# A hybrid decoder step: where squares, sampled states and recurrence chunks stand in the order

## The chip, the cores and the metric

The kernel runs on one core of a Trainium2 chip. The time is device microseconds (us) of one execution, from the first to the last instruction and what lies around them; a run is given by its median. A core has five engines that work side by side, each through its own instructions in a fixed order: TensorE (PE: matmuls and transposes), VectorE (DVE), ScalarE (ACT), GpSimd (POOL) and SyncE (SP, which issues most of the transfers). POOL and ACT issue transfers too.

## The reference

One layer of a hybrid decoder on 512 prompt tokens and 8 sampled tokens, width 1024, in float32. One combined projection of the normalised input feeds two branches: a retention (4 heads, keys of 256, values of 512, chunks of 128 tokens) and an RWKV-7 time mixing (16 heads of 64). Each branch has a SiLU gate and its own down projection; sigmoid gates merge them.

```python
h = _rmsnorm(x, norm_g)
P = einsum('btd,dn->btn', concat([h_prev, h]), w_in)[:, 1:]     # all projections
# retention, per head; s0 is zero for the prompt, state_ret for the samples
inner = einsum('bhid,bhjd->bhij', qc, kc) * dmask
o = einsum('bhij,bhjv->bhiv', inner, vc) + einsum('bhid,bhdv->bhiv', qc * q_dec, s)
s = chunk_dec * s + einsum('bhjd,bhjv->bhdv', kc * k_dec, vc)
# RWKV-7, per token
sk = einsum('bhvk,bhk->bhv', s, kk_t)
s = s * w_t - sk * (a_t * kk_t) + v_t * k_t
o = einsum('bhvk,bhk->bhv', s, r_t)
```

After the merge follow an output projection and residual, a per-layer embedding with a gate, and a final norm. The outputs are the tokens, both branches' new states and the shift rows.

## The kernel before, in words

**Products.** Activations and weights are split into a high and a low half (`hhi`/`hlo`, `whi`/`wlo`, `yahi`/`yalo`, `ybhi`/`yblo`), and each product is three matmuls: high by high, high by low, low by high. A weight comes by SP into `raw` (three buffers, L142), ACT copies it to `whi` (L147) and DVE subtracts for `wlo` (L148); `whi` and `wlo` have two buffers each, so a new copy waits until PE has done with the weight before the last one. `mm_half` (L160) runs the matmuls over one half of the tokens (256 or 264 columns) into a PSUM tile `ph`, one of four.

**Stages.** (1) Prologue: the four token tiles `xt` of 128 tokens and the samples' `xs` are squared by ACT (`sumsq`, L263), the inverse root is taken by 13 small DVE instructions (`inv`, L178 to L186), the rows are scaled (L270), transposed by PE (L278) and split (L282, L283), tokens 0 to 255 by `transposed(0)`, the rest by `transposed(1)`. (2) The RWKV projections and what the recurrence needs, pair of heads by pair (to 262 us). (3) The four retention heads (to 707 us): keys and queries with rotation (`rx`, L801), values (`phv`, L838, with the samples' `vsm`, L831), scores, the gates `gs` (L891), `sampled(h)`, the outputs. `sampled(h)` loads the 8 samples' states of a head in four tiles `tS` of 1 MB by POOL (L758), scales them by the decay on ACT (L764, 16 copies), adds the new outer product on DVE (L765), reads them by PE (L770) and stores them. (4) The RWKV recurrence, 8 chunks of 64 tokens, each a chain over all engines: products `UO` (L1025), the solve `U` (L1034), the state's step `dS` (L1040), `UO` again (L1043), the outputs `Ot` copied by ACT (L1056). Between the chunks' steps lie *fills*: eight merge gates `mg` (stored to MBd by SP) and then eight output tiles of the first down projection, `down_a` (weights of the retention's output `ya`; results `ua`, stored to UAd). (5) The second down projection, down_b, on the recurrence's output: `yb` is written to YBd tile by tile, loaded again by SP (L1149) when stage 5 begins, and split (L1150, L1151). (6) Output projection, embedding, final norm.

**What sets the order.** The program is written out once; a scheduler then simulates the engines and lays each engine's instructions in an order, by priorities (`tc.high_priority(offset=...)`, a larger offset goes first) and by `tc.issue_after(i)`, which lets nothing in its block be taken up before instruction `i` in the order. `after(a, b)` is a true dependency. On the chip, each engine then keeps the order it was given, whatever comes late. In stage 4 the table `AT` says how many fills have been written by the time chunk c is: chunk c follows fill number AT[c].

Of the kernel before, what the change touches and what calls it, by code (L numbers as in the profile page):

```python
# [8 lines left out]
F32 = mybir.dt.float32  # L9
F32R = mybir.dt.float32r  # L10
I32 = mybir.dt.int32
AF = mybir.ActivationFunctionType
# [5 lines left out]
T, B8, NT = 512, 8, 520  # L18
# [7 lines left out]
DV = 512  # L26
# [53 lines left out]
def body(tc, A, O, dbg=None, upto="Z"):  # L80
# [3 lines left out]
    act, dve, pe, sp, pool = nc.scalar, nc.vector, nc.tensor, nc.sync, nc.gpsimd  # L84
# [7 lines left out]
    with es:  # L92
# [51 lines left out]
        def weights(src, keep=None, ready=None):  # L144
            raw, ld = ready or fetch(src)
            hi, lo = keep or [wp.tile([128, KT, 128], F32R, tag=t, name=t, bufs=2) for t in ("whi", "wlo")]
            cp = act.activation(hi, raw, AF.Copy)  # L147
            sb = dve.tensor_tensor(lo, raw, hi, ALU.subtract)  # L148
            marks[:] = [getattr(i, "ins", i) for i in (ld, sb, cp)]
            return hi, lo  # L150
# [110 lines left out]
        def sumsq(x, r_, n):  # L261
            junk = p0.tile([128, D], F32, tag="junk", name="junk", bufs=2)
            act.activation(junk[0:r_], x, AF.Square, accum_out=ssq[0:r_, n:n + 1])  # L263
# [8 lines left out]
        def transposed(g):  # L272
            for q in range(4):
                ps = (bank("pht") if q < 3 else pq.tile([128, 512], F32, tag="po", name="pht")).rearrange("p (k t) -> p k t", k=2)
                for n in range(2):
                    for i in range(2):
                        k = 2 * q + i
                        pe.transpose(ps[:, i, n * 128:(n + 1) * 128], xts[2 * g + n][:, k * 128:(k + 1) * 128], ident)  # L278
                for i in range(2):
                    k = 2 * q + i  # L280
                    cs = slice(256 * g, 256 * g + 256)
                    hi = act.activation(hhi[:, k, cs], ps[:, i], AF.Copy, scale=ng[:, k:k + 1])  # L282
                    last = dve.scalar_tensor_tensor(hlo[:, k, cs], ps[:, i], ng[:, k:k + 1], hhi[:, k, cs], ALU.mult, ALU.subtract)  # L283
            return [getattr(i, "ins", i) for i in (hi, last)]
# [6 lines left out]
        with tc.issue_after(getattr(last, "ins", last)):  # L291
            pre = [weights(None, ready=raws[0])]
        with tc.high_priority(offset=10000):
            sumsq(xs[0:8], 8, 4)
            for n in (2, 3):
                sumsq(xts[n], 128, n)
            with tc.issue_after(getattr(last, "ins", last)):
                inv(2, 5)
                scaled(xts[2], 128, 2, act)
                scaled(xts[3], 128, 3)  # L300
                scaled(xs[0:8], 8, 4)
        last = transposed(0)
        with tc.issue_after(last[0]), tc.issue_after(last[1]):
            pre.append(weights(None, ready=raws[1]))
        ps = bank("phs")
        psv = ps[:, 0:KT * 16].rearrange("p (k b) -> p k b", b=16)
        for k in range(KT):
# [437 lines left out]
        dve.tensor_tensor(s8, s8, i4[:, 2], ALU.add)  # L745
        dve.tensor_tensor(sum8, s8, i4[:, 3], ALU.add)

        def sampled(h):
            qz = pR.tile([128, 2, 4, 34], F32, tag="qz", name="qz", bufs=1)
            dve.memset(qz, 0.0)  # L750
            dve.tensor_copy(qz[:, :, :, 0], qs[:, h, :, 0:4])
            dve.tensor_copy(qz[:, :, :, 33], qs[:, h, :, 4:8])
            po = pq.tile([128, 512], F32, tag="po", name="po")
            for g in range(2):
                Ss = []
                for i in range(2):
                    S = pT.tile([128, 4, NT], F32, tag="tS", name="tS", bufs=4)[:, :, 0:DV]
                    pool.dma_start(S, A["state_ret"][0, 4 * g:4 * g + 4, h, 128 * i:128 * i + 128, :].rearrange("b p v -> p b v"))  # L758
                    Ss.append(S)
                for b in range(4):  # L760
                    vb = bank("vb")
                    pe.matmul(vb, sel[:, 4 * g + b, :], vsr, start=True, stop=True)  # L762
                    for i, S in enumerate(Ss):
                        act.activation(S[:, b, :], S[:, b, :], AF.Copy, scale=GAM[h])  # L764
                        last = dve.scalar_tensor_tensor(S[:, b, :], vb, ks[:, h, i, 4 * g + b:4 * g + b + 1], S[:, b, :], ALU.mult, ALU.add)  # L765

                for i, S in enumerate(Ss):
                    n_ = 32 if g == 0 and i == 0 else 2
                    for b in range(4):
                        m_ = pe.matmul(po[32 * b:32 * b + n_, :], qz[:, i, b, 32 * g:32 * g + n_], S[:, b, :],  # L770
                                       start=(n_ == 32), stop=(g == 1 and i == 1), skip_group_check=True)
                        if b == 0 and i == 0:
                            after(m_, last)
                    pool.dma_start(O[5][0, 4 * g:4 * g + 4, h, 128 * i:128 * i + 128, :].rearrange("b p v -> p b v"), S)
            return po

        def sampled_out(h, po):
# [6 lines left out]
            for i in range(4):  # L784
# [3 lines left out]
                              ps.rearrange("p (i b r) -> p i b r", i=4, b=4)[:, :, :, 0:2],  # L788
                              gs8[:, hs_, :].rearrange("p i (g b) -> p i b g", g=2), ALU.mult)

        OFF = [0, 512, 896, 1152]
        GBC = [0, 0, 0, 4, 8]
        for h in range(H):
# [33 lines left out]
            for j in range(4):  # L827
                ready = fetch(w_in[256 * j:256 * j + 256, O_V + DV * h:O_V + DV * h + DV])
                raws, w = raws[-1:] + [wide(ready[0])], [wide(t) for t in weights(None, ready=ready)]
                if j % 2:  # L830
                    ms = [pe.matmul(vsm[32 * g:32 * g + 32], hst[:, 2 * j - 2 + g, :], raws[g // 2][:, g % 2, :],  # L831
                                    start=(j == 1), stop=(j == 3), skip_group_check=True) for g in range(4)]
                    side_by_side(ms)
                    after(ms[0], marks[2])
                for jt in range(4):
                    for k in range(2):
                        for x, (w_, r) in enumerate(((w[0], hhi), (w[0], hlo), (w[1], hhi))):
                            m_ = pe.matmul(vps[jt], r[:, 2 * j + k, 128 * jt:128 * jt + 128], w_[:, k, :],  # L838
                                           start=(j == 0 and k == 0 and x == 0), stop=(j == 3 and k == 1 and x == 2))
                tail[:] = [getattr(m_, "ins", m_)]  # L840
                advance("v")
            vhi = pB.tile([128, 4, DV], F32R, tag="vhi", name="vhi")
            vlo = pB.tile([128, 4, DV], F32R, tag="vlo", name="vlo")
# [35 lines left out]
            for jt in range(4):  # L879
# [2 lines left out]
                    pe.transpose(ps[:, 128 * i:128 * i + 128], kf[i][:, 128 * jt:128 * jt + 128], ident)  # L882
                act.activation(dhi[:, jt, :], ps[:, 0:256], AF.Copy, scale=kdec[:, h, jt:jt + 1])
                dve.scalar_tensor_tensor(dlo[:, jt, :], ps[:, 0:256], kdec[:, h, jt:jt + 1], dhi[:, jt, :], ALU.mult, ALU.subtract)
            po = sampled(h)

            gs = []
            for i in range(4):
                g = pB.tile([128, NT], F32, tag="vg", name="gs", bufs=4)
                for (j, c0, c1), ps in zip(HV, proj(w_in[:, col(O_GA + DV * h, i)], hhi, hlo)):  # L890
                    act.activation(g[:, c0:c1], ps, AF.Silu)  # L891
                act.activation(gs8[:, 4 * h + i, :], g[:, T:NT], AF.Copy)
                gs.append(g)
                advance("gate")
                if h == H - 1 and i == 2:
                    ya_tiles(h, pT)
                    ya_load(0, pT, pool)
# [199 lines left out]
            loads(1)  # L1097
        done = []
        nxt_y = beside_rwkv(128, slice(0, 128))
        AT = [0, 3, 6, 8, 9, 11, 12, 13, 16]  # L1100
        for c in range(NCH):
            with tc.high_priority(offset=20000):
                PS = chunk(c)
            if c % 2 == 1:
                x = (Ot, 128, slice((c - 1) * C, (c + 1) * C))
                with tc.high_priority(offset=10000):
                    finish_rwkv(*x)
                done.append((c + 1, x))
            for _ in range(AT[c + 1] - AT[c]):
                next(fl)  # L1110
            if c + 2 < NCH:
                with tc.issue_after(marks[0]), tc.high_priority(offset=20000):
                    loads(c + 2)
            if done and c == done[0][0]:
                with tc.high_priority(offset=10000):
                    emit_rwkv(*done.pop(0)[1], *nxt_y)
                nxt_y = beside_rwkv(128, slice(c * C, c * C + 128)) if c != 4 else beside_rwkv(B8, slice(T, NT))
            if c == 4:
                o8 = pC.tile([128, 16, C], F32, tag="Ot", name="o8", bufs=2)[0:B8]
                pool.dma_start(o8, OSd.rearrange("(b h) v -> b h v", h=16))  # L1120
                x = (o8, B8, slice(T, NT))
                finish_rwkv(*x)
                emit_rwkv(*x, *nxt_y)
                nxt_y = beside_rwkv(128, slice(c * C, c * C + 128))
# [205 lines left out]
```

## Time and profile before

| | |
|---|---|
| median of 3 runs | 1075.98 us (1072.61 to 1078.3) |
| profiled execution | 1071.51 us, span 1069.7 us |
| PE busy | 1042.0 us of the span, 97% |
| mean granted clock of PE | 0.992 |
| weight copies `whi` on ACT / `wlo` on DVE | 135 x 1.06 us / 135 x 1.22 us |
| transfers | 199.45 MB, 186 GB/s over the span |

A row of the time line has the start, the length, the engine (SPq is SP's queue of transfers), the line of the kernel, what is written from what, the shapes, the count and, in brackets, how long the engine stood idle before and what released it. PE is busy nearly everywhere, so what counts is where it stands idle, and how the engines that feed it are ordered just before.

### The profile page before, as it was taken

The numbers are of one execution on the slowest core, as the hardware profiler recorded it, in microseconds if no ns is written. First come the engines' busy times: TensorE is split into PE (matmuls) and PEld (weight loads), VectorE is DVE, ScalarE is ACT, GpSimd is POOL, SyncE is SP. The second block draws the span as 40 slices with busy tenths as digits, with TensorE's granted clock in tenths as the row PEclk, the third lists the DMA queues.
The fourth block names the chain that finished last, engine by engine and source line by source line (L and its number), as shares of the span: only waits on it lengthen the run. The fifth ranks groups of instructions, "written<-read, shape, count | busy, mean of one in ns | idle before, by whom it ended". The sixth has DMA issues, their size and how long they took to land.

```text
span 1069.7 us, 22049 instructions
## 1 busy us (share of the span) xinstructions
PE 1042.0 (97%) x8932; PEld 974.8 (91%) x8932; DVE 785.2 (73%) x1429; ACT 494.8 (46%) x973; POOL 79.5 (7%) x139
## 2 busy tenths in 40 slices
PE   7999999999999999999999999998999999999995
PEld 6999989999879788987989889898999999999995
DVE  6647989884499699949894698864777755666875
ACT  6744565544464543373445333354323224334554
POOL 2000110100300200010010000110001100000000
PEclk8999999999999999999999999999999999999998
DMA  5623488788943943493288633969996649643222
GB/s 182 179 80 99 122 191 223 188 246 228 330 160 90 327 146 99 144 319 103 86 310 229 230 115 112 328 198 330 309 283 214 171 145 302 206 119 100 81 59 81
DMA packets 239224, 199.45 MB, mean 186 GB/s; under 512 B 58988, under 2 KB 203225, under 8 KB 237970
## 3 DMA queue, kind: packets, MB, share of 16 engines
q1 hardware_dynamic: 225586, 149.60, 47.7%
q0 software_dynamic: 13376, 48.17, 13.2%
q8 instruction: 70, 1.15, 0.4%
q14 instruction: 32, 0.26, 0.1%
q10 hardware_dynamic: 160, 0.27, 0.1%
HBM read 137.70 MB, written 60.00 MB: 185 GB/s over the span
## 4 chain that ended last, share of the span: by engine, by line
PE 85%; DMA 6%; DVE 3%; ACT 2%; issue 1%; SPq 1%; POOL 0%; DVEq 0%; POOLq 0%; ACTq 0%
PE ph L160 58%; PE phv L838 8%; PE o L910 3%; PE st L921 2%; PE sc L863 1%; PE po L770 1%; PE g L506 1%; PE UO L1025 1%; DMA raw<-in_w_ple_gate_dram 1%; DMA raw<-in_w_in_dram 1%; DMA yalo<-YAd 1%; DMA BKt<-BKd 1%; DMA MBd<-mg 1%; PE vb L762 1%; PE vsm L831 1%
## 5 line engine op out<-in xcount | busy, mean ns | idle before, releaser
L160 PE MATMUL ph<-hhi,whi 128*128 128x256 f32 (+2 forms) x1296 | 370.5, 286 | 0.9 <-ACT hhi L282 0.4
L160 PE MATMUL ph<-hlo,whi 128*128 128x256 f32 (+2 forms) x1296 | 369.4, 285 | 0.2 <-DVE hlo L283 0.2
L160 PE MATMUL ph<-hhi,wlo 128*128 128x256 f32 (+2 forms) x1296 | 368.8, 285 | 0.5 <-DVE wlo L148 0.5
L160 PEld LDWEIGHTS ph<-hhi,whi 128*128 128x128 f32 x1296 | 244.2, 189 | 6.1 <-issue 1.7
L160 PEld LDWEIGHTS ph<-hhi,wlo 128*128 128x128 f32 x1296 | 245.0, 189 | 2.2 <-DVE wlo L148 0.7
L160 PEld LDWEIGHTS ph<-hlo,whi 128*128 128x128 f32 x1296 | 244.5, 189 | 1.9 <-DVE hlo L283 0.7
L147 ACT ACTIVATE whi<-raw 128x1024 fp32r<-128x1024 f32 x135 | 142.9, 1059 | 208.9 <-PE ph L160 154.2
L148 DVE TENSOR_TENSOR wlo<-raw,whi 128x1024 fp32r<-128x1024 f32 x135 | 164.8, 1221 | 86.4 <-ACT whi L147 85.4
L160 PE MATMUL ph<-yalo,whi 128*128 128x256 f32 (+1 forms) x256 | 72.4, 285 | 0.0
L160 PE MATMUL ph<-yahi,whi 128*128 128x256 f32 (+1 forms) x256 | 72.2, 284 | 0.0
L160 PE MATMUL ph<-yahi,wlo 128*128 128x256 f32 (+1 forms) x256 | 71.9, 285 | 0.0
L623 DVE TENSOR_TENSOR tm<-M 128x62 f32<-128x62 f32 (+30 forms) x62 | 52.9, 853 | 0.6
L625 DVE TENSOR_TENSOR M<-M,tm 128x62 f32<-128x62 f32 (+30 forms) x62 | 52.8, 852 | 0.6
L838 PE MATMUL phv<-whi,hhi 128*128 128x512 f32 x128 | 51.5, 403 | 0.0
L838 PE MATMUL phv<-whi,hlo 128*128 128x512 f32 x128 | 50.5, 395 | 0.0
L160 PEld LDWEIGHTS ph<-yalo,whi 128*128 128x128 f32 x256 | 48.1, 188 | 0.3
L160 PEld LDWEIGHTS ph<-yahi,whi 128*128 128x128 f32 x256 | 48.1, 188 | 0.2
L160 PEld LDWEIGHTS ph<-yahi,wlo 128*128 128x128 f32 x256 | 47.8, 188 | 0.3
L838 PE MATMUL phv<-wlo,hhi 128*128 128x512 f32 x128 | 46.8, 395 | 0.5 <-DVE wlo L148 0.5
L765 DVE SCALAR_TENSOR_TENSOR tS<-vb,ks,tS 128x512 f32<-128x512 f32 x64 | 44.1, 742 | 3.3 <-PE vb L762 3.3
L764 ACT ACTIVATE tS<-tS 128x512 f32<-128x512 f32 x64 | 35.0, 620 | 12.5 <-DMA tS<-in_state_ret_dram 12.4
L215 ACT ACTIVATE mg<-ph 128x256 f32<-128x256 f32 (+1 forms) x48 | 17.7, 378 | 41.2 <-PE ph L160 20.6
(454 smaller groups left out, 2120.0 us busy)
## 6 DMA issues: line engine op xcount, KB each, us to landing
raw<-in_w_in_dram SPq DMA_DIRECT2D x97, 512.0 KB, 5.0
tS<-in_state_ret_dram POOLq DMA_DIRECT2D x16, 1024.0 KB, 8.4
out_dram<-tS POOLq DMA_DIRECT2D x16, 1024.0 KB, 9.9
KR<-KRd SPq DMA_DIRECT2D x8, 1024.0 KB, 9.5
raw<-in_w_down_a_dram SPq DMA_DIRECT2D x16, 512.0 KB, 6.8
KRd<-KRS SPq DMA_DIRECT2D x16, 256.0 KB, 4.5
KRd<-GM SPq DMA_DIRECT2D x16, 256.0 KB, 4.8
BKt<-BKd SPq DMA_DIRECT2D x8, 512.0 KB, 9.9
```

The lines of the kernel that those rows point to most:

```text
L147: cp = act.activation(hi, raw, AF.Copy)
L148: sb = dve.tensor_tensor(lo, raw, hi, ALU.subtract)
L160: m_ = pe.matmul(ps[:, 0:c1 - c0], w[:, k, :], r[:, k0 + k, c0:c1], start=(x == 0), stop=(x == n_ - 1))
L215: act.activation(g[:, c0:c1], ps, fn, scale=scale)
L506: ms = [pe.matmul(gs[2 * q + hh][:, c * 128:(c + 1) * 128], BK[hs_, 4 * q + c, :], KRS[hs_, 4 * q + c, :], start=True, stop=True) for q in ...
L623: dve.tensor_tensor(tv, M[:, 0:s, s:s + 1].to_broadcast([128, s, n]), M[:, s:s + 1, s + 1:C].to_broadcast([128, s, n]), ALU.mult)
L625: dve.tensor_tensor(M[:, 0:s, s + 1:C], M[:, 0:s, s + 1:C], tv, ALU.add)
L764: act.activation(S[:, b, :], S[:, b, :], AF.Copy, scale=GAM[h])
L765: last = dve.scalar_tensor_tensor(S[:, b, :], vb, ks[:, h, i, 4 * g + b:4 * g + b + 1], S[:, b, :], ALU.mult, ALU.add)
L838: m_ = pe.matmul(vps[jt], r[:, 2 * j + k, 128 * jt:128 * jt + 128], w_[:, k, :], start=(j == 0 and k == 0 and x == 0), stop=(j == 3 and k ...
L910: pe.matmul(ps, a_[:, o_:o_ + 128], b_[:, jt, :], start=(x == 0), stop=(x == len(seq) - 1))
L921: pe.matmul(ps, a_[:, jt, 128 * i:128 * i + 128], b_[:, jt, :], start=(x == 0), stop=(x == 11))
```

## The change

**A, prologue.** `transposed(0)` for tokens 0 to 255 is written, with priority, ahead of the squares of the other tokens and the samples. These squares come after its last ACT split (`last[0]`), their inverse root and scaling after its last DVE split (`last[1]`), and the second weight is split after both.

**B, sampled states.** `sampled(h)` is divided: `sampled_states(h)` issues the loads, `sampled(h, SS)` does the rest. Head 0's loads depend on PE's products with V's second and fourth weight (`vmark`), and its work is written behind the first gate's copy of the sampled columns. For the other heads the two stand one behind the other as before.

**C, recurrence.** `AT` goes from [0, 3, 6, 8, 9, 11, 12, 13, 16] to [0, 6, 8, 9, 10, 11, 12, 13, 16], and each chunk but the first may be taken up only behind the last matmul of the fills written before it (`tail[0]`).

```diff
         with tc.high_priority(offset=10000):
-            sumsq(xs[0:8], 8, 4)
+            last = transposed(0)
+        with tc.issue_after(last[0]), tc.issue_after(last[1]):
+            pre.append(weights(None, ready=raws[1]))
+        with tc.high_priority(offset=9000), tc.issue_after(last[0]):
             for n in (2, 3):
                 sumsq(xts[n], 128, n)
-            with tc.issue_after(getattr(last, "ins", last)):
+            sumsq(xs[0:8], 8, 4)
+            with tc.issue_after(last[1]):
                 inv(2, 5)
                 scaled(xts[2], 128, 2, act)
                 scaled(xts[3], 128, 3)
                 scaled(xs[0:8], 8, 4)
-        last = transposed(0)
-        with tc.issue_after(last[0]), tc.issue_after(last[1]):
-            pre.append(weights(None, ready=raws[1]))
...
-        def sampled(h):
+        def sampled_states(h):
+            Ss = []
+            for g in range(2):
+                for i in range(2):
+                    S = pT.tile([128, 4, NT], F32, tag="tS", name="tS", bufs=4)[:, :, 0:DV]
+                    ld = pool.dma_start(S, A["state_ret"][0, 4 * g:4 * g + 4, h, 128 * i:128 * i + 128, :].rearrange("b p v -> p b v"))
+                    if h == 0:
+                        after(ld, vmark[g])
+                    Ss.append(S)
+            return Ss
...
+                if j % 2:
+                    vmark.append(m_)
...
-            po = sampled(h)
+            SS = sampled_states(h)
+            if h:
+                po = sampled(h, SS)
...
-                act.activation(gs8[:, 4 * h + i, :], g[:, T:NT], AF.Copy)
+                a_ = act.activation(gs8[:, 4 * h + i, :], g[:, T:NT], AF.Copy)
                 gs.append(g)
+                if h == 0 and i == 0:
+                    with tc.issue_after(getattr(a_, "ins", a_)):
+                        po = sampled(h, SS)
...
-        AT = [0, 3, 6, 8, 9, 11, 12, 13, 16]
+        AT = [0, 6, 8, 9, 10, 11, 12, 13, 16]
         for c in range(NCH):
-            with tc.high_priority(offset=20000):
+            with ExitStack() as cs_:
+                if c:
+                    cs_.enter_context(tc.issue_after(tail[0]))
+                cs_.enter_context(tc.high_priority(offset=20000))
                 PS = chunk(c)
```

What this makes of the engines' orders is seen at three places. Line numbers of the changed kernel are up to 19 higher.

ACT in the prologue, `-` as it was and `+` as it is now; `junk` are the squares, `hhi` the split of `transposed(0)`, `whi` the copy of the second weight:

```order
+L282 ACTIVATE hhi<-pht,ng 128x256 x8
+L263 ACTIVATE junk,ssq<-xt 128x1024 x2
+L147 ACTIVATE whi<-raw 128x1024
 L263 ACTIVATE junk,ssq<-xs 8x1024
-L263 ACTIVATE junk,ssq<-xt 128x1024 x2
-L282 ACTIVATE hhi<-pht,ng 128x256 x8
-L147 ACTIVATE whi<-raw 128x1024
 L270 ACTIVATE xt<-xt,rs 128x1024
```

The eight splits now stand ahead of the squares, and one square stands behind the second weight's copy.

ACT in the V products of head 0, as it was; `rx` is the copy of a key's or query's product, `whi` in the third row from the end the copy of V's second weight, which `vsm` and the products behind it wait for:

```order
L801 ACTIVATE rx<-ph 128x256
L764 ACTIVATE tS<-tS 128x512 x4
L147 ACTIVATE whi<-raw 128x1024
L801 ACTIVATE rx<-ph 128x264
L764 ACTIVATE tS<-tS 128x512 x8
```

and now, first at the same place, then behind the first gate's copy of the sampled columns (`gs_66<-gs`):

```order
L810 ACTIVATE rx<-ph 128x256
L147 ACTIVATE whi<-raw 128x1024
L810 ACTIVATE rx<-ph 128x264
L822 ACTIVATE qhi<-m_3894 128x512
L824 ACTIVATE qs<-m_3894 128x8
...
L905 ACTIVATE gs_66<-gs 128x8
L772 ACTIVATE tS<-tS 128x512 x15
L894 ACTIVATE dhi<-kt,kdec 128x256
L772 ACTIVATE tS<-tS 128x512
L904 ACTIVATE gs<-ph 128x256
L879 ACTIVATE ihi<-s__4152 128x128
L147 ACTIVATE whi<-raw 128x1024
```

The scalings of the states have left the V products and stand, all 16, between the first gate and the copies of the second gate and of the next weight.

SP where down_a ends and down_b begins, as it was; `raw` are down_b's weights, `ua` and `UAd` down_a's tiles, `yb` the recurrence's output:

```order
L142 DMA raw<-in_w_down_b_dram 128x8x128
L1074 DMA ua<-MAd 128x520
L142 DMA raw<-in_w_down_b_dram 128x8x128
L1149 DMA yb<-YBd 128x8x128
L1077 DMA UAd<-ua 128x520
L1149 DMA yb<-YBd 128x8x128 x2
L1149 DMA yb<-YBd 128x8x8
L1161 DMA xn<-in_x_prompt_dram 128x512 x2
```

and now:

```order
L142 DMA raw<-in_w_down_b_dram 128x8x128
L1090 DMA ua<-MAd 128x520
L142 DMA raw<-in_w_down_b_dram 128x8x128
L1093 DMA UAd<-ua 128x520
L142 DMA raw<-in_w_down_b_dram 128x8x128 x2
L1093 DMA UAd<-ua 128x520
L142 DMA raw<-in_w_down_b_dram 128x8x128
L1168 DMA yb<-YBd 128x8x128 x3
L1168 DMA yb<-YBd 128x8x8
L1180 DMA xn<-in_x_prompt_dram 128x512 x2
```

The loads of `yb` stand behind the store of down_a's last tile and behind the third, fourth and fifth weight of down_b. On PE the number of down_a's matmuls between the second transpose `so` (the recurrence's final state) and down_b has gone from 135 to 17; between chunk 7's last `UO` and down_b from 353 to 233. Ahead of chunk 1's `UO` there are now 48 matmuls of the merge gates, where there were none.

More of the change, by code (lines that the diff above doesn't have):

```diff
@@ L746, in body, with sampled @@
         dve.tensor_tensor(sum8, s8, i4[:, 3], ALU.add)
-        def sampled(h):
+        def sampled_states(h):
[8 more added lines that the diff above has]
+            return Ss
+        def sampled(h, SS):
             qz = pR.tile([128, 2, 4, 34], F32, tag="qz", name="qz", bufs=1)
@@ L754, in sampled @@
             for g in range(2):
[L755 to L759, printed above, removed]
+                Ss = SS[2 * g:2 * g + 2]
                 for b in range(4):
@@ L789, in sampled_out @@
                               gs8[:, hs_, :].rearrange("p i (g b) -> p i b g", g=2), ALU.mult)
+        vmark = []
         OFF = [0, 512, 896, 1152]
```

## The prediction

> **What bounds the kernel now.** I read the busy times first, then the chain that ended last, then the list of what TensorE waited for. The page's busy times and chain:
>
> ```profile
> PE 1042.0 (97%) x8932; PEld 974.8 (91%) x8932; DVE 785.2 (73%) x1429; ACT 494.8 (46%) x973; POOL 79.5 (7%) x139
> PE 85%; DMA 6%; DVE 3%; ACT 2%; issue 1%; SPq 1%; POOL 0%; DVEq 0%; POOLq 0%; ACTq 0%
> ```
>
> TensorE (PE) is busy 1042.0 of 1069.7 us, so an edit can win only from the 27.7 us in which PE does nothing, and it loses whatever new idle time it makes. The waits of PE, by line and releaser (us in total, times, longest):
>
> ```profile
> PE UO L1025 <- ACT Ot L1056: 3.4, 3, 2.7
> PE vsm L831 <- issue: 2.6, 1, 2.6
> PE g L506 <- ACT a L455: 1.4, 2, 0.7
> PE g L506 <- ACT sg L455: 1.1, 1, 1.1
> ```
>
> Three edits, five places: I go through them in order of time, each against the profiled execution.
>
> **1. The prologue (edit A): +1.3 us.** ScalarE (ACT), VectorE (DVE) and PE rows of the prologue:
>
> ```profile
> 10.76 1.04 ACT L263 ACTIVATE junk<-xt 128x1024 f32<-128x1024 f32 x1
> 11.80 3.13 ACT L282 ACTIVATE hhi<-pht,ng 128x256 fp32r<-128x256 f32 x8
> 14.79 1.08 ACT L147 ACTIVATE whi<-raw 128x1024 fp32r<-128x1024 f32 x1
> 18.29 1.15 ACT L270 ACTIVATE xt<-xt,rs 128x1024 f32<-128x1024 f32 x1 [2.41 <-DVE rs L186]
> 15.91 1.23 DVE L148 TENSOR_TENSOR wlo<-raw,whi 128x1024 fp32r<-128x1024 f32 x1
> 17.05 0.15 DVE L184 TENSOR_TENSOR nt<-rs 128x3 f32<-128x3 f32 x1
> 18.03 0.16 DVE L186 SCALAR_TENSOR_TENSOR rs<-nt,rs 128x3 f32<-128x3 f32 x1
> 21.28 0.60 PE L278 MATMUL pht<-ident,xt 128*128 128x128 f32 x4
> ```
>
> Before, the squares (junk) end at 11.8 and hhi runs to 14.9. DVE's steps of the inverse root slip in between the hlo copies, the last six from 17.05 to 18.03, 0.2 us apart; the ACT scaling of token tile 2 ends at 19.44, before PE asks for it at 21.28. With the new order ACT runs hhi when its transposes come (about 11.55 to 14.7), then two squares (2 x 1.0, to 16.6), then the second whi (1.08, to 17.7), then the sample's square (to 18.8). Only then can DVE start the inverse root: 13 instructions of some 0.2 us, to 21.4; the scaling takes 1.15, to 22.55. PE's transposes of tokens 2 and 3 start at 22.6 in place of 21.28: **+1.3**. Bounds: +0.4, if the 13 steps take the 0.15 us of their rows (0.65 less) and the squares start 0.25 sooner; +2.0, if the second weight's later wlo (17.7 to 18.9, before 15.9 to 17.1) comes on top.
>
> **2. Pairs before the heads: -1.0.** The scheduler has also moved some ACT copies by one or two places around the three waits of L506 (2.5 us in all); in two of them the awaited copy `a` now stands ahead of a weight copy of 1.06 us. I take -1.0, with bounds -2.5 and 0 (the wait passes to the next operand).
>
> **3. V of head 0 (edit B): -2.6, and +0.7 given back.** ACT and PE rows:
>
> ```profile
> 287.78 0.37 ACT L801 ACTIVATE rx<-ph 128x256 f32<-128x256 f32 x1
> 291.71 2.19 ACT L764 ACTIVATE tS<-tS 128x512 f32<-128x512 f32 x4 [3.56 <-DMA tS<-in_state_ret_dram]
> 293.81 1.04 ACT L147 ACTIVATE whi<-raw 128x1024 fp32r<-128x1024 f32 x1
> 294.95 1.06 PE L831 MATMUL vsm<-raw,hst 128*32 128x512 f32 x8 [2.64 <-issue]
> ```
>
> The releaser says "issue", but whi ends at 294.85 and PE starts 0.1 us later: ACT sits 3.56 us on a state that is still in transfer, then scales it for 2.19, and the weight copy that PE needs stands behind. The new order has the copy straight behind rx, near 288.7, and PE does not stop: **-2.6** (bounds -1.6, if the copy still waits for its buffer; -3.2, if the next L838 wait of 0.5 on wlo goes too). The 16 scalings do not vanish: they now stand behind the first gate's copy of the sampled columns.
>
> ```profile
> 326.46 0.21 ACT L892 ACTIVATE gs<-gs 128x8 f32<-128x8 f32 x1
> 331.50 1.06 ACT L147 ACTIVATE whi<-raw 128x1024 fp32r<-128x1024 f32 x1 [0.61 <-PE ph L160]
> 337.93 1.06 ACT L147 ACTIVATE whi<-raw 128x1024 fp32r<-128x1024 f32 x1 [2.41 <-PE ph L160]
> ```
>
> 16 x 0.55 = 8.8 us (2.19 for four) from 326.7 hold ACT until 335.5. Behind them stand a copy out of gate 1 and the whi that is taken at 331.50 now; it would end at about 337.7 and its wlo at 338.9. The gate that uses it starts when the gate before frees its weights, 337.9 (the <-PE of the last row). So PE waits up to 1.0: I take **+0.7**, bounds 0 and 2.
>
> **4. Start of the recurrence (edit C, chunk held behind fills): 0.** ACT and PE rows, then the windows (PE, PEld, DVE, ACT, POOL busy, the granted clock, DMA share):
>
> ```profile
> 735.12 2.19 ACT L646 ACTIVATE yahi<-yalo 128x512 fp32r<-128x512 f32 x4 [5.35 <-DMA yalo<-YAd]
> 738.29 1.18 ACT L215 ACTIVATE mg<-ph 128x256 f32<-128x256 f32 x4
> 737.85 3.59 PE L1025 MATMUL UO<-SV,KR 128*64 128x64 f32 x64 [2.73 <-ACT Ot L1056]
> ```
>
> ```profile
> 294.00:296.00 2.00, 1.05 (x9) 0.24 (x9) 1.12 (x1) 2.00 (x4) 0.00 (x0) 1.00 1.03 397
> 736.00:738.00 2.00, 0.15 (x2) 0.15 (x4) 1.94 (x4) 2.00 (x6) 0.00 (x0) 0.95 1.10 362
> 738.00:740.00 2.00, 2.00 (x40) 2.00 (x42) 1.67 (x5) 2.00 (x7) 0.00 (x0) 0.50 0.99 300
> 740.00:742.00 2.00, 2.00 (x34) 1.78 (x30) 2.00 (x4) 2.00 (x4) 0.00 (x0) 0.70 1.01 342
> ```
>
> Now 48 fill matmuls (5.8 us) stand where chunk 1's first product waited 2.73 us. They do not fill the hole: their PSUM buffers are the four that the mg copies of 738.29 empty, and these stand behind the same yahi copies, with the same late transfer ahead. PE would stop at 735.12 until about 738.5, 3.4 in place of 2.73, with the same clock loss behind, and the small later wait of chunk 2 on Ot (0.6) goes. Net **0**, bounds -4.9 (stall 2.7, clock 1.6 and 0.6 all gone) and +1.
>
> **5. End of the recurrence and of down_a (edit C): +11.3 idle, +1.6 clock.** This is where the sum is decided. Chunks 2 to 7 each stand later among the fills: behind chunk 7's last product there were 353 matmuls of down_a, now 233, and behind the second final transpose (so) 135, now 17. PE, ACT, DVE and SP rows of this place now:
>
> ```profile
> 879.96 0.60 PE L1133 MATMUL so<-ident,PS 128*64 128x128 f32 x4
> 896.49 0.28 PE L160 MATMUL ph<-yahi,wlo 128*128 128x264 f32 x1
> 890.11 1.06 ACT L1150 ACTIVATE ybhi<-yb 128x1024 fp32r<-128x1024 f32 x1 [3.80 <-DMA yb<-YBd]
> 892.54 1.06 ACT L1150 ACTIVATE ybhi<-yb 128x1024 fp32r<-128x1024 f32 x1 [0.30 <-DMA yb<-YBd]
> 896.69 1.06 ACT L147 ACTIVATE whi<-raw 128x1024 fp32r<-128x1024 f32 x1 [0.80 <-PE ph L160]
> 893.64 1.23 DVE L1151 TENSOR_TENSOR yblo<-yb,ybhi 128x1024 fp32r<-128x1024 f32 x1
> 897.78 1.23 DVE L148 TENSOR_TENSOR wlo<-raw,whi 128x1024 fp32r<-128x1024 f32 x1 [0.31 <-ACT whi L147]
> 884.63 0.37 SPq L142 DMA_DIRECT2D raw<-in_w_down_b_dram  x1
> 885.22 0.41 SPq L1149 DMA_DIRECT2D yb<-YBd  x1
> 887.01 3.63 SPq L1149 DMA_DIRECT2D yb<-YBd  x3
> 897.67 0.38 SPq L1077 DMA_DIRECT2D UAd<-ua  x1
> ```
>
> The yb loads are issued 11.4 us ahead of down_a's end E (896.6), land 4.9 to 5.5 us later, and are split by 894.9: just in time. In the changed program SP has ahead of them the store of down_a's last tile and three more down_b weights. The store needs down_a's last product (now 897.67, E+1.1). The last of the weights needs the buffer whose wlo ends with the copy that E itself releases: whi E+0.1, wlo E+1.2 to E+2.4 (896.69 and 897.78 now). So yb goes out at E+3.0 (0.59 behind the weight, as 884.63 to 885.22), the second yb at E+3.5. It lands 5.5 later, E+9.0; ybhi 1.06 and yblo 1.23 behind it (892.54, 893.64) end near E+11.4. On PE only down_b follows those 17 matmuls, and its first group needs both token tiles: PE is idle some **11.3 us**. Bounds: 8.4, if the weight's buffer were free and only the store held yb (E+1.2, then 4.9 to land and 2.3 to split); 14, if the transfer takes 8 us behind a weight.
>
> After this PE starts cold. In the trace 2.73 us of waiting cost 0.05, 0.50 and 0.30 of three 2 us windows: 0.1 + 1.0 + 0.6 = 1.7 us, of which I take **1.6**; bounds 1 and 3. The Trainium skill, "TensorE: Matmul & The Clock Gate" (Part 1: The HAM clock gate), states half the clock after an idle window of about 3.4 us, for about 3.4 us: by it the loss would be 1.7 as well. This trace differs in the threshold: 2.73 us were enough at 738, 2.64 us were not at 294 (clock 1.00).
>
> **Sum.** 1.3 - 1.0 - 2.6 + 0.7 + 0 + 11.3 + 1.6 = +11.3: 1071.5 becomes 1082.8. The profiled execution lies 4.5 below the median of the three runs, so by the median 1075.98 + 11.3 = **1087.3**.
>
> **The rivals.** *Not slower:* down_b's input is there in time. The place is SP's queue ahead of yb, the price point 5, and it decides if yb is issued before about E-8. It would need both the last weight's buffer and the last tile's store free long before E. For it: today yb leaves at E-11.4, behind a weight too. Against it: the store holds the product of E by its data. Then 12.9 fall away: 1087.3 - 12.9 = 1074.4; with the chunk start's bound of -4.9 it would be 1069.5.
> *The hole at 735 is filled* (point 4 at its bound): 48 matmuls run while ACT waits. For it, they need neither yahi nor Ot; against it, the four buffers. 1087.3 - 4.9 = 1082.4.
> *Transfers slower* at the end of down_a: with weights, yb, x and merge tiles all released at once, yb takes 8 us or more, and the clock stays low. 1087.3 + 5 = 1092.
>
> **Chances.** Half a per cent, 5.4 us, is about what a measurement of this kernel tells from no change. The forecast 0.62 (own range 1081 to 1092), nearly all slower. Yb in time 0.20: half of it faster, nearly half no change. Hole filled 0.12: half slower, half no change. Slow transfers 0.06, slower. That makes slower 0.70, same 0.18, faster 0.12. The range takes in the hole filled and most of yb in time: 1072 to 1093.
>
> **What would show it.** In the new profile: the wait of UO on Ot gone from the list and a wait of ph on mg in its place near 735 (4); no wait of vsm (3); a wait of pht for xt of about 1.3 near 21 (1); above all, a wait of ph on ybhi or yblo of about 11 us where down_a ends, SP issuing yb behind the last UAd store, and a clock slice under 1.00 there (5). If PE runs from down_a into down_b without a gap, the prediction is wrong in its main term.

## The result and the profile after

The changed kernel takes 1091.44 us (median of 4 runs, 1087.77 to 1092.4), the kernel before 1075.97 on the same chip (4 runs): ratio 1.014, 95% interval 1.0104 to 1.0176, 15.5 us slower. The profiled execution took 1091.09 us; that of before, at 1071.51, was a quick one, so the two traces lie 19.6 apart.

Busy times and granted clock of the page after:

```profile
span 1089.3 us, 22049 instructions
PE 1048.6 (96%) x8932; PEld 977.5 (90%) x8932; DVE 788.7 (72%) x1429; ACT 493.2 (45%) x973; POOL 80.1 (7%) x139
PEclk9999999999999999999999999999999997999998
```

PE has the same 8932 matmuls, is busy 6.6 us more and idle 40.7 us in place of 27.7. One slice of the clock, near 910 us, stands at 7. What PE waited for (us in total, times, longest):

```profile
PE ph L160 <- ACT ybhi L1169: 11.6, 1, 11.6
...
PE ph L160 <- ACT mg L215: 2.8, 1, 2.8
PE ph L160 <- DVE wlo L148: 1.4, 3, 0.8
PE phv L847 <- ACT whi L147: 1.2, 1, 1.2
...
PE ph L160 <- ACT whi L147: 0.9, 1, 0.9
PE xt L1183 <- DMA xn<-in_x_prompt_dram: 0.9, 1, 0.9
```

The first row is new, and of the rows shown it is four times as long as the next (a row of 3.5 us at the kernel's start, left out between them, is in both kernels): the first product of down_b waits for the split of `yb`. Around it, in the time line, PE, SP, ACT and DVE:

```profile
898.16 0.60 PE L1152 MATMUL so<-ident,PS 128*64 128x128 f32 x4
900.55 0.28 PE L160 MATMUL ph<-yahi,wlo 128*128 128x264 f32 x1
912.44 0.58 PE L160 MATMUL ph<-ybhi,whi 128*128 128x256 f32 x1 [11.61 <-ACT ybhi L1169]
913.70 0.58 PE L160 MATMUL ph<-yblo,whi 128*128 128x256 f32 x1 [0.68 <-DVE yblo L1170]
...
901.32 0.34 SPq L1093 DMA_DIRECT2D UAd<-ua  x1
903.09 0.37 SPq L142 DMA_DIRECT2D raw<-in_w_down_b_dram  x1
903.68 5.83 SPq L1168 DMA_DIRECT2D yb<-YBd  x4
904.22 2.21 SPq L1168 DMA_DIRECT2D yb<-YBd  x1
...
911.33 1.06 ACT L1169 ACTIVATE ybhi<-yb 128x1024 fp32r<-128x1024 f32 x1 [0.63 <-DMA yb<-YBd]
...
901.84 1.23 DVE L148 TENSOR_TENSOR wlo<-raw,whi 128x1024 fp32r<-128x1024 f32 x1 [0.55 <-ACT whi L147]
912.42 1.23 DVE L1170 TENSOR_TENSOR yblo<-yb,ybhi 128x1024 fp32r<-128x1024 f32 x1 [0.47 <-ACT ybhi L1169]
```

SP issues the store of the last tile at E+0.5 (E = 900.83, the end of down_a), the last weight when its buffer's `wlo` ends (903.07) and `yb` behind it at E+2.85. (The row at 904.22 is the second of the four loads, looked at by itself.)

SP's queue is not all that holds this load. `yb` lies in memory that the recurrence uses up to its end, and in the program its first load waits for the last transpose `so`. That row ends at 898.76, 2.1 us ahead of E; in the kernel before it ended 16.2 us ahead (880.56 and 896.77). From the start of the row to the first load it took 5.3 us before and takes 5.5 now. So the load has not moved away from the end of the recurrence; the end of the recurrence has moved towards E.

The clock there (PE, PEld, DVE, ACT, POOL busy, PEclk, DMA share, GB/s):

```profile
904.00:908.00 4.00, 0.00 (x0) 0.00 (x0) 0.42 (x3) 0.31 (x1) 0.00 (x0) 0.50 0.99 281
912.00:914.00 2.00, 0.88 (x2) 0.59 (x3) 1.23 (x1) 1.13 (x2) 0.00 (x0) 0.50 0.98 246
914.00:916.00 2.00, 2.00 (x10) 2.00 (x10) 1.36 (x2) 0.46 (x2) 0.00 (x0) 0.50 1.05 345
916.00:918.00 2.00, 2.00 (x14) 2.00 (x14) 0.00 (x0) 0.00 (x0) 0.00 (x0) 0.67 1.01 368
```

Busy time times the share of the clock that is missing: 0.44 + 1.0 + 0.66 = 2.1 us lost. With the two waits, 11.61 and 0.68, and the 0.89 on `xn` behind, that makes 15.3 us in this one place.

To see the rest, I cut each trace at six matmuls that every version has: the first `pss` of the pairs (47.7 us in the trace of before), the transposes `g` of the samples behind the pairs (263.0), head 1's first V product (387.3), the last head's `yas` (706.9), down_a's last product (896.5) and the last `hold` of the final norm (1059.1). The table gives what each stage took longer than in the profiled execution of before. A, B and C are the three edits as named under the change.

| us | prologue | pairs | head 0, V | heads 1-3 | recurrence, down_a | rest | sum |
|---|---|---|---|---|---|---|---|
| changed kernel | +2.2 | +1.5 | -1.4 | +3.4 | -1.7 | +15.5 | +19.6 |
| e1, A alone | +2.8 | +1.5 | +2.6 | 0.0 | +1.2 | +0.6 | +8.6 |
| e2, B alone | +1.2 | 0.0 | +2.4 | +2.6 | +2.9 | +0.5 | +9.7 |
| e3, C alone | -1.2 | 0.0 | +2.7 | 0.0 | +0.9 | +16.4 | +18.8 |
| e4, A and B | +0.9 | +1.5 | -2.4 | +3.1 | -0.8 | +0.8 | +3.1 |
| e5, hold with the old table | +1.5 | 0.0 | +4.4 | 0.0 | +2.4 | +14.6 | +23.0 |
| e6, `yb` by POOL | +1.5 | +1.5 | -2.9 | +3.4 | -3.0 | +18.9 | +19.4 |
| e7, hold, chunks earlier | +1.7 | +1.5 | +0.8 | +2.8 | +0.3 | +2.6 | +9.7 |
| e8, A, weight first | +0.7 | -0.1 | +3.4 | 0.0 | +0.7 | +2.4 | +7.0 |
| e9, B, `vsm` together | -1.2 | 0.0 | -1.7 | +0.2 | +0.3 | +0.6 | -1.8 |
| e10, e9 and fills on DVE | +1.3 | 0.0 | -3.1 | +0.9 | +1.5 | +0.1 | +0.6 |
| e11, e10 and hold, chunks earlier | -0.7 | 0.0 | -2.8 | +1.2 | +0.1 | +4.1 | +1.8 |

Each line is one execution. Versions whose order there is alike lie up to 3 us apart in the prologue and up to some 5 in head 0 and in the recurrence; in the pairs and heads 1 to 3 they lie within 1 us. So a column is read over all lines, and the medians of the runs decide on a whole version.

### The profile page after: what moved, and what is told of

Same layout as the page of the kernel before. It is cut to its first block, busy times and chain, and to the rows that moved or that the text cites. A ratio compares the mean times of both kernels' runs of the same rounds, so it can differ in the third digit from the quotient of the medians.

```text
span 1089.3 us, 22049 instructions
## 1 busy us (share of the span) xinstructions
PE 1048.6 (96%) x8932; PEld 977.5 (90%) x8932; DVE 788.7 (72%) x1429; ACT 493.2 (45%) x973; POOL 80.1 (7%) x139
## 4 chain that ended last, share of the span: by engine, by line
PE 70%; DMA 9%; issue 8%; DVE 6%; ACT 4%; SPq 2%; POOL 0%; DVEq 0%; POOLq 0%; ACTq 0%
PE ph L160 50%; PE phv L847 4%; PE o L926 2%; SPq L630 2%; DVE wlo L148 1%; PE UO L1041 1%; PE st L937 1%; DMA raw<-in_w_ple_gate_dram 1%; PE g L507 1%; DMA yalo<-YAd 1%; DMA raw<-in_w_in_dram 1%; PE po L778 1%; ACT whi L147 1%; DMA tS<-in_state_ret_dram 1%; PE sc L874 1%
## 5 line engine op out<-in xcount | busy, mean ns | idle before, releaser
L160 PE MATMUL ph<-yahi,whi 128*128 128x264 f32 (+1 forms) x256 | 73.0, 286 | 0.0
L160 PE MATMUL ph<-yalo,whi 128*128 128x264 f32 (+1 forms) x256 | 72.8, 285 | 0.0
L160 PE MATMUL ph<-ybhi,whi 128*128 128x264 f32 (+1 forms) x128 | 37.4, 292 | 11.6 <-ACT ybhi L1169 11.6
```

Source lines behind the costliest of these rows:

```text
L160: m_ = pe.matmul(ps[:, 0:c1 - c0], w[:, k, :], r[:, k0 + k, c0:c1], start=(x == 0), stop=(x == n_ - 1))
```

## The experiments

### One part alone, and two together

**A alone.**

```diff
...
+            last = transposed(0)
+        with tc.issue_after(last[0]), tc.issue_after(last[1]):
+            pre.append(weights(None, ready=raws[1]))
+        with tc.high_priority(offset=9000), tc.issue_after(last[0]):
             for n in (2, 3):
                 sumsq(xts[n], 128, n)
+            sumsq(xs[0:8], 8, 4)
...
```

> Edit A alone. My theory (the second weight's copy and split, now behind two squares, stop TensorE in the first products, and the later scaling does the rest): 2.3 us more, with two new waits of some 0.9 and 0.8 us for the second weight near 18 and 19 us; the last transposes of tokens 256 to 511 start 2.3 us later. Rival (the prologue's delay is taken back in the pairs, whose copies stand in another order): no change. If the 1.4 us that the pairs lost come with A's order as well, 3.7 us more.

1081.2 us (6 runs) against 1074.99 (21 runs): 1.0051, 1.0023 to 1.008, so 5.5 us more by the ratio, 2.5 to 8.6 by its interval; the 3.7 expected with the pairs' loss lie inside. PE's waits in its prologue:

```profile
18.24 0.39 PE L160 MATMUL ph<-hhi,whi 128*128 128x256 f32 x1 [0.92 <-ACT whi L147]
19.50 0.38 PE L160 MATMUL ph<-hhi,wlo 128*128 128x256 f32 x1 [0.76 <-DVE wlo L148]
```

PE does not stop for the late token tile but, earlier, for the second weight, which now stands behind two squares: 1.7 us. The 1.5 us in the pairs came with A; I had expected them only as a condition.

**B alone.**

```diff
-            po = sampled(h)
+            SS = sampled_states(h)
+            if h:
+                po = sampled(h, SS)
...
+                if h == 0 and i == 0:
+                    with tc.issue_after(getattr(a_, "ins", a_)):
+                        po = sampled(h, SS)
```

> Edit B alone. My theory (the wait of TensorE for V's second weight goes, nothing else is lost but a short wait behind the 16 scalings): 2 to 2.6 us less. Rival 1 (GpSimd's late fill of the selection tile holds ScalarE ahead of V's first weight, as in the changed kernel, so half comes back): 1 to 1.5 us less. Rival 2 (the heads run slower with the loads put later, the 3.4 us that the changed kernel lost between head 0's V and the heads' end): 2 us more.

A miss: 1077.06 us (10 runs), 1.0019, 0.9996 to 1.0042, so no gain where 2 to 2.6 us less were expected; the second rival, 2 us more, was nearest. The wait of `vsm` is gone, but in its profile a wait for V's first weight stands in its place (PE, then ACT and POOL):

```profile
291.30 0.80 PE L846 MATMUL phv<-whi,hhi 128*128 128x512 f32 x1 [2.89 <-ACT whi L147]
...
287.42 2.13 ACT L735 ACTIVATE sel<-ident 8x1024 fp32r<-8x1024 f32 x2 [6.06 <-POOL sel L731]
...
283.24 3.18 POOL L668 DMA_DIRECT2D sv<-SMd  x6 [26.35 <-PE ph L160]
286.41 0.97 POOL L731 MEMSET sel<- 128x1024 f32 x1
```

POOL takes 3.18 us to issue six loads of the samples' columns, then zeroes `sel`; ACT waits 6.06 us for that, and the weight's copy stands behind it. This chain is in the kernel before as well, and how late it comes differs from one execution to the next: e9, the same in this place, waits 0.9. Heads 1 to 3 lost 2.6 us.

**C alone.**

```diff
-        AT = [0, 3, 6, 8, 9, 11, 12, 13, 16]
+        AT = [0, 6, 8, 9, 10, 11, 12, 13, 16]
...
+                if c:
+                    cs_.enter_context(tc.issue_after(tail[0]))
```

> Edit C alone. My theory (the loss is the wait for the second down projection's input at the end of the first): TensorE waits 11 to 12 us for ybhi and yblo, with a clock loss of 2 behind it, and nothing is lost before 700 us: 12 to 15 us more than before. Rival (a good part of the changed kernel's loss comes from the edits before the recurrence): 8 to 10 us more.

1090.11 us (4 runs): 1.0126, 1.0096 to 1.0157, nearly all of the loss.

```profile
911.35 0.58 PE L160 MATMUL ph<-ybhi,whi 128*128 128x256 f32 x1 [12.19 <-ACT ybhi L1153]
```

The wait for `yb` comes with C and without A and B.

**A and B, without C.**

> Edits A and B without C. My theory (C holds nearly all of the loss): the input of the second down projection is there in time, no wait of TensorE between the down projections; 0 to 2 us more than before (2.3 of the prologue, less 1.4 or more of V). Rival (the 5.7 us by which the changed kernel's heads end late are A's and B's own): 4 to 6 us more.

1076.92 us (10 runs): 1.0019, 0.9992 to 1.0046. PE goes from down_a to down_b without a wait. So the ratios add up: 0.19% for A and B and 1.26% for C make 1.45%, and all three together measured 1.40%. A alone and B alone do not add up like that, 0.51% and 0.19% against 0.19% for both. Why is not settled; in the profiles it is head 0 that differs, +2.6 and +2.4 us against -2.4.

### Which half of C, and by what

**The hold with the old table.** Only `issue_after(tail[0])` is put in; AT stays.

> The hold of edit C alone, with the old table of fills. My theory (the hold moves chunk 7 to the end, since each chunk waits for the fills dealt before it; behind the second final transpose stand 17 matmuls here too): TensorE waits 11 to 12 us where the second down projection begins; 13 to 16 us more than before. Rival (the new table makes the loss): no wait there, within 3 us of before.

1087.24 us (4 runs) against 1074.41 (19 runs): 1.011, 1.0067 to 1.0152.

```profile
917.03 0.58 PE L160 MATMUL ph<-ybhi,whi 128*128 128x256 f32 x1 [11.91 <-ACT ybhi L1153]
```

The hold does it, with either table. (The new table alone, without the hold, gives every engine the same order as the old one, so it was not run.) Without the hold the scheduler takes a chunk up as soon as its operands allow, whatever AT says; with it, AT is obeyed, and chunk 7 is taken up only behind the thirteenth fill.

**The same, with earlier chunks.** The whole change, but

```diff
-        AT = [0, 6, 8, 9, 10, 11, 12, 13, 16]
+        AT = [0, 6, 7, 8, 9, 10, 11, 12, 16]
```

> The changed kernel with chunks 2 to 7 dealt one fill earlier each: 104 matmuls behind the second final transpose in place of 17. My theory (the distance from the end of the recurrence to the end of the first down projection decides): the input is loaded in time, a wait of 0 to 1.5 us there, 14 to 16 us less than the changed kernel, level with edits A and B alone. Rival (the hold costs as such, by its shape of the recurrence): 5 to 10 us less only.

1079.74 us (10 runs): 1.0042, 1.0016 to 1.0067, so 1.0% (10.5 us, some 5 either way) less than the changed kernel, by chunks 2 to 7 one fill earlier. I had expected 14 to 16. Behind the last transpose `so` there are now 105 matmuls of down_a, not 17. PE at that transpose, SP, and PE at the start of down_b:

```profile
890.71 0.60 PE L1152 MATMUL so<-ident,PS 128*64 128x128 f32 x4
...
894.67 0.37 SPq L142 DMA_DIRECT2D raw<-in_w_down_b_dram  x1
895.26 6.42 SPq L1168 DMA_DIRECT2D yb<-YBd  x4
...
904.99 0.39 PE L160 MATMUL ph<-ybhi,whi 128*128 128x256 f32 x1 [1.08 <-ACT ybhi L1169]
```

`yb` still stands behind a weight, and it leaves 4.6 us after the start of that row in place of 5.5. But down_a now ends at 903.91, 13.2 us after it in place of 2.7, and 1.08 us are left of the wait, with 1.18 on `xn` behind it.

**The load of `yb` on another queue.** The whole change, but

```diff
-                sp.dma_start(src, YBd[:, :, cols].rearrange("k r n -> r k n"))
+                pool.dma_start(src, YBd[:, :, cols].rearrange("k r n -> r k n"))
```

> The changed kernel with the loads of the second down projection's input issued by GpSimd in place of SyncE. My theory (3 us of the wait are the place in SyncE's queue, behind a weight whose buffer only the end of the first down projection frees; the rest is the final transposes, the transfer and the split): issue near the end of the first down projection in place of 2.9 us behind it, a wait of 8 to 9 us in place of 11.6, 3 to 4 us less than the changed kernel. Rival (the transfers share the engines with the weights, so the place in the queue decides nothing): wait 11 to 12 us, same time as the changed kernel.

A miss: 1092.52 us (4 runs), 1.0147, 1.0114 to 1.0181, no better than the changed kernel. Issue, ACT, PE and landing (count, KB, median us):

```profile
896.90 3.51 POOL L1168 DMA_DIRECT2D yb<-YBd  x4
912.30 0.38 ACT L1193 ACTIVATE pthi<-pt 128x256 fp32r<-128x256 f32 x1 [5.67 <-PE pt L1192]
912.58 2.14 ACT L1169 ACTIVATE ybhi<-yb 128x1024 fp32r<-128x1024 f32 x3
909.87 1.97 PE L1183 MATMUL xt<-ident,xn 128*128 128x128 f32 x8 [12.66 <-DMA xn<-in_x_prompt_dram]
913.68 0.58 PE L160 MATMUL ph<-ybhi,whi 128*128 128x256 f32 x1 [1.42 <-ACT ybhi L1169]
yb<-YBd POOLq DMA_DIRECT2D x3, 512.0 KB, 8.0
```

and the changed kernel's row of the same transfer:

```profile
yb<-YBd SPq DMA_DIRECT2D x3, 512.0 KB, 5.9
```

The median of SP's row holds the first load alone. By the moments at which each load signalled its landing in the trace, SP's three took 5.9, 7.1 and 6.8 us from issue to landing, POOL's 7.0, 8.0 and 9.0. The first load left at the end of down_a (897.21) in place of 2.85 us later, but took longer to land; and the orders had changed as well. On PE, transposes of `xn` stand ahead of down_b and wait for a load of their own, and on ACT the split of the second tile stands behind `pthi`, which waits for the transposes `pt` that follow them. So the run does not isolate SP's queue. The second tile had landed 8.6 us after down_a's end (905.77), and in the changed kernel it was split at 10.5. By an estimate from these two times, SP's order costs 1 to 2 of the 11.6 us; no run shows it by itself.

### The smaller terms

**A, with the weight first.** A alone, and the squares of tokens 256 to 511 behind the second weight's copy too:

```diff
-        with tc.high_priority(offset=9000), tc.issue_after(last[0]):
+        with tc.high_priority(offset=9000), tc.issue_after(last[0]), tc.issue_after(marks[2]):
```

> Edit A alone, but with the second weight's copy ahead of the squares. Theory of the prediction (the late squares delay the inverse root and the scaling, so the last transposes start late): the two waits for the second weight go, a wait of 1 to 2 us for the scaled tokens takes their place near 21 to 22 us, and the prologue ends 1 to 2.5 us later than before. Rival (the second weight behind the squares is the whole loss): the prologue ends within 0.5 us of before, 2 us less than A alone.

1078.11 us (10 runs): 1.0018, 0.9992 to 1.0044. The waits for the weight are gone, and the one that I had forecast for the changed kernel is there:

```profile
22.57 0.66 PE L278 MATMUL pht<-ident,xt 128*128 128x128 f32 x4 [1.19 <-ACT xt L270]
```

And the pairs are back to -0.1: their +1.5 comes with the order that A as written sets off, not with the earlier transposes as such.

**B, with `vsm` kept together.** In heads 1 and 2 B's order has the four `vsm` matmuls of one step of V as two pairs, six products apart. B alone, and

```diff
+                    with tc.high_priority(offset=10000):
-                    ms = [pe.matmul(vsm[32 * g:32 * g + 32], ...) for g in range(4)]
+                        ms = [pe.matmul(vsm[32 * g:32 * g + 32], ...) for g in range(4)]
```

> Edit B alone, with the four samples' value matmuls (vsm) kept together by a priority. My theory (B wins some 3 us in head 0 and loses 3 in the heads 1 to 3, of which 2 are two groups of vsm that the new order splits into pairs; a pair takes as long as the four side by side): all groups run in 1.0 us, the time from head 1's V to the heads' end is 2 us shorter than with B, and the whole 1.5 to 3 us less than before. Rival (the loss in the heads is not vsm's, for example the later states): heads as long as with B, whole within 1 us of before.

1074.77 us (12 runs) against 1076.58 (28 runs): 0.9979, 0.9959 to 1.0. Heads 1 to 3: +0.2 in place of +2.6 to +3.4. The group in this version, then in the changed kernel (four matmuls are eight records):

```profile
389.13 1.07 PE L840 MATMUL vsm<-raw,hst 128*32 128x512 f32 x8
```

```profile
394.35 1.05 PE L840 MATMUL vsm<-raw,hst 128*32 128x512 f32 x4
396.92 1.05 PE L840 MATMUL vsm<-raw,hst 128*32 128x512 f32 x4
```

Four matmuls that each use 32 of the array's columns take as long as two of them.

**The fills of `sel`, `vsr` and `hst` on DVE.** On top of that, `pool.memset` becomes `dve.memset` for these three.

> The kernel of the run before, with the fills of the selection tile, of vsr and of hst on VectorE in place of GpSimd. My theory (GpSimd's late fill holds ScalarE ahead of V's first weight; this cost 1.2 to 2.9 us in several runs and none in the one of before): no wait of TensorE for V's first weight, 1 to 2 us less than the run before, 3 to 5 less than before. Rival (VectorE's own work there is delayed as much): no change against the run before.

1075.17 us (11 runs): 0.9977, 0.9957 to 0.9996. V's first weight is no longer waited for, and head 0 is at its lowest of all lines, -3.1; on the median it makes no difference to e9, where I had expected 1 to 2 us; the rival was right.

**And the hold, with early chunks.** On top of that, the hold and AT = [0, 6, 7, 8, 9, 10, 11, 12, 16].

> The kernel of the run before with edit C's hold and the table with chunks 2 to 7 one fill earlier. My theory (the hold neither wins nor loses much where chunk 7 ends early enough: the stall at the recurrence's start passes from UO to ph): within 2 us of the run before. Rival 1 (the hold wins the wait at the recurrence's start, 2.7 us and its clock loss): 3 to 5 us less than the run before. Rival 2 (104 matmuls behind the final transposes are too few): a wait of 1 to 3 us at the second down projection, 3 us more than the run before.

1073.73 us (12 runs): 0.9971, 0.9954 to 0.9989. This is the lowest median, 0.3% below the kernel before and, by the ratios, 1.7% below the changed one; from e10 and e9 these runs can't tell it. It has the wait of C's order at the start of the recurrence and about a quarter of C's price (+4.1 in the rest):

```profile
736.77 0.58 PE L160 MATMUL ph<-hhi,whi 128*128 128x256 f32 x1 [4.03 <-ACT mg L215]
895.52 0.38 PE L160 MATMUL ph<-ybhi,whi 128*128 128x256 f32 x1 [1.02 <-ACT ybhi L1169]
```

## Why the prediction was right, and where it was not

The verdict, the mechanism that carries it and its place were right: slower, by the input of down_b, at the end of down_a. The measured median lies 4.1 us above the forecast, because the terms beside it were off and the main one was some 2 us short. That it is not more is in part luck: by the columns B won more than forecast, and that stands against losses that the sum did not have.

**Point 1, prologue, +1.3: the size right, the place not.** The five profiles with A as written lie 1.6 above the seven with the old prologue, that of before among them (1.8 against 0.2 where PE, behind the last transposes, takes `vrow`; single profiles scatter by 1). That difference is known to about 1 us. But in the changed kernel PE stops for the second weight (0.90 and 0.76 us) and then no longer for `xt`; I had the weight's later `wlo` as an upper bound on top. PE that stopped at 18 comes to 21 late enough, or nearly: in e4, e6 and e7 0.56 to 0.58 us of waiting for `xt` came on top. e8 shows the forecast wait, 1.19, once the weight is out of the way.

**Point 2, pairs, -1.0: wrong in sign.** It measured +1.5 in each of the five versions with A as written and 0.0 or -0.1 in all others. The waits I looked at did shrink:

```profile
PE g L507 <- ACT sg L456: 1.1, 1, 1.1
PE g L534 <- DVE BK L529: 0.9, 1, 0.9
PE g L507 <- ACT a L456: 0.6, 2, 0.3
PE pb L492 <- DVE GM L513: 0.4, 1, 0.4
```

1.7 us in place of 2.5 on L507; but 1.3 us of other waits came up, on DVE. The step that failed is to read a gain from three waits while the same reordering moved what stands around them. About 1 us of the 1.5 has no row of its own, and its cause stays open.

**Point 3, head 0: -2.6 and +0.7.** The wait of `vsm` went as forecast: 1.5 to 3.3 us, 2.4 on average, in the five profiles without B (before's own among them), and none in the six with it, those with the fills on DVE left aside. In the whole stage the five lie on average 2.6 above before's and the six 0.9 below, so B brings 3.5 by the columns. With a scatter of up to 5 us in either group that is not told apart from the 1.9 forecast. The 16 scalings stand where I had them, and the weight behind them held PE for 0.2 us, not 0.7:

```profile
329.53 7.91 ACT L772 ACTIVATE tS<-tS 128x512 f32<-128x512 f32 x15
341.04 0.39 PE L160 MATMUL ph<-hhi,wlo 128*128 128x256 f32 x1 [0.19 <-DVE wlo L148]
```

What I did not see is that this stage of before is itself uneven, by POOL's late fill of `sel`; the profile of before happened to have none of that wait, and the changed kernel's has 1.2 us.

**The missing term: heads 1 to 3, +3.** I took the order there as unchanged. B's smaller body moved the four `vsm` apart in two heads: 2 x 1.0 us, taken back by e9. What is left, about 1 us, is not explained; e9 stands at +0.2, but e10 and e11, with the same groups whole, at +0.9 and +1.2.

**Point 4, start of the recurrence, 0: right.** The wait of UO on Ot became one of `ph` on `mg`, for the reason given (the four PSUM buffers behind the copies of `yahi`):

```profile
743.65 0.58 PE L160 MATMUL ph<-hhi,whi 128*128 128x256 f32 x1 [2.79 <-ACT mg L215]
```

Over all profiles PE's waits from 706 to 800 us sum to 2.2 to 4.3 us with the hold and 2.9 to 5.2 without it, so no gain or loss by the 48 fills or the hold stands out there.

**Point 5, end of down_a, +12.9: right, undersized by some 2 us.** The idle time is 11.6, 12.2 and 11.9 in the changed kernel, e3 and e5, for 11.3; the first `yb` left at E+2.85, for E+3.0, and the second at E+3.4, for E+3.5. The sum was short elsewhere. The second load's issue took 2.2 us, not 0.5, and it landed 7.1 us after its start, not 5.5; so its split began at E+10.5, not E+9.0. `yblo`'s end came a second time on the path (0.68). The clock cost 2.1, for 1.6, and `xn` behind it 0.9. The rival *transfers slower* came out nearest to the measured time, but by its number more than by its cause: none of the three loads took the 8 us that it asks for.

By the columns (the 3.1 is the mean of the five versions with `vsm` pulled apart, the 15 the rest of the changed kernel, e3 and e5 less that of the versions without the hold), 1.6 + 1.5 - 3.5 + 3.1 + 0 + 15 = 17.7 us against 11.3 forecast; the medians say 15.5, within 11 to 19.

The rival *yb in time* fell for the reason named against it, the store of the last tile and the weight behind it, and for one that I had not named: the load must wait for the last `so`, and that ends only 2.1 us ahead of E. Freeing SP's queue alone would not have made it hold. e7 shows what does: with 105 matmuls behind `so`, the load leaves 8.7 us ahead of down_a's end, close to the E-8 that the rival asks for. The rival *hole filled* fell too; the wait is still there.

## What to carry to other kernels

When an edit moves a chain of work towards the end of a stage, look for the loads of the next stage that must wait for that chain, and count how many matmuls are left behind it to cover them: here 135 covered the load, 17 left 11.6 us of waiting, 105 left 1.1. A place in the queue behind the store of the stage's last result comes on top, here by the smaller part. Making a scheduler obey a table that it could go round is a change of its own: the table has to be tuned again for it. And an edit that only takes work out of one place can pull apart instructions elsewhere that are cheap only side by side, so compare the whole order, not the places that the edit names.

## What the runs showed of the hardware

**Columns side by side.** Two `vsm` matmuls on 32 columns each took 1.05 us, four took 1.07: pulling them apart cost a full microsecond each time, and no row shows idle time for it.

**The same load by two queues.** The three loads of 512 KB of `yb` took 5.9, 7.1 and 6.8 us to land when SP issued them and 7.0, 8.0 and 9.0 when POOL did. The Trainium skill, "DMA: Bandwidth & Descriptors" (Specifications), gives a first-byte latency of about 1 us for GpSimd's path and 0.6 for SyncE's; the direction agrees, but the 1 to 2 us measured here are more, and POOL's loads left some 3 us earlier, with other transfers beside them.

**The clock.** After 11.6 us of idle time PE ran at 0.50 until past 916 and at 0.67 in the window behind, 2.1 us lost; near 744 a wait of 2.79 us also led to a window of 0.50:

```profile
742.00:744.00 2.00, 0.35 (x1) 0.35 (x2) 1.97 (x4) 2.00 (x7) 0.00 (x0) 0.81 1.12 351
744.00:746.00 2.00, 2.00 (x11) 2.00 (x11) 2.00 (x5) 2.00 (x6) 0.00 (x0) 0.50 1.13 355
746.00:748.00 2.00, 2.00 (x16) 2.00 (x16) 2.00 (x4) 1.44 (x2) 0.00 (x0) 0.84 0.98 362
```

0.07 + 1.0 + 0.32 make 1.4 us: a wait of 2.8 us cost two thirds of the clock that one of 11.6 did.

**Scatter.** The kernel before took 1070.5 to 1082.0 us over the runs. In the profiles the differences between like versions lie in the prologue, at the start of V (POOL's loads and fill) and at the start of the recurrence (PE's waits of 2.2 to 5.2 us).
